# Attention scores: the low parts of the keys in one tile per key-value head, with zeros in the other 64 rows

## The chip, the cores and the metric

The kernel runs on one core of a Trainium2 chip. The metric is the device time of one execution in microseconds (us); of several executions the median is taken. A profiled execution gives, besides, a trace: every instruction of each engine with its start and its length. The engines are PE (TensorE: matmuls, and PEld, the loads of their stationary operand), DVE (VectorE), ACT (ScalarE), POOL (GpSimd) and SP, which here issues the transfers (DMA).

## What is computed

One layer of a decoder for a prompt of 1024 tokens and 8 single-token samples that share the weights. The part that the change touches is the sliding-window attention of the prompt: 8 query heads, 2 key-value heads, 64 channels a head, blocks of 128 queries against the 256 keys of their own and the previous block.

```python
def split_in(h, w_in, q_norm, k_norm):
    z = h @ w_in
    ...
    q = rms_norm(q.reshape(*lead, N_HEADS, HEAD_DIM), q_norm)
    k = rms_norm(k.reshape(*lead, N_KV_HEADS, HEAD_DIM), k_norm)
    ...
def sink_attention(q, k, v, mask, sinks):
    ...
    s = jnp.einsum("nqkgd,nskd->nkgqs", qg, k).astype(jnp.float32) * (HEAD_DIM ** -0.5)
    s = jnp.where(mask, s, NEG)
    ...
    p = jnp.exp(s - m)
    denom = jnp.sum(p, axis=-1, keepdims=True) + jnp.exp(sink - m)
    o = jnp.einsum("nkgqs,nskd->nqkgd", (p / denom).astype(v.dtype), v)
```

Before it stand an RMS norm and the input projection, behind it the gates, the output projection and a SwiGLU.

## The kernel before, in words

Every float32 matrix is kept as a rounded high part and a low part (the remainder), and a product is made of the terms high·high, high·low and low·high. In the helper `mm` (L204 to L211) these are three matmuls that add up in one bank.

The tokens are cut in three chunks of 264, 384 and 384 columns. In the first stage the input is turned (`turn`, L333), its low and high parts go to `hTl` and `hTh`, and a copy `xT` of each turned tile (L345, on ACT) is stored to `xscr` in HBM (L348, issued by SP) for the residual much later. `xT` has a pool of 8 buffers: copy n needs the buffer that the transfer of copy n-8 has read. The norm's factors come from a short chain of POOL operations (`rsqrt`, L115), are spread over the partitions by a matmul (L360) and copied to `bc` by ACT (`norm_bc`, L366). `do_k`, `do_v` and `do_q` multiply their projections by `bc` on DVE (for k: `kr`, L388), and PE turns `kr` (L395, `pkt`).

For attention, `QA[j]` and `QB[j]` hold in one 128-row tile the high part of a query head in the 64 rows of its kv head and the low part in the other 64. `Kh[kv]` holds the key's high part twice, in both halves. `Kl` holds the low parts of both kv heads in one tile, head 0 in rows 0 to 63 and head 1 in rows 64 to 127. So in `att_scores` one matmul with 128 rows (L606) gives q_high·k_high + q_low·k_high, and a second one with 64 rows (L607) adds q_high·k_low.

There are 16 units (8 blocks, 2 kv heads), each with 4 pairs of such matmuls. The table `FILLS` puts groups of 24 matmuls of the projections (`pq`, `pu`, `pg`) between them. A unit goes through scores (PE), mask and maximum (DVE, L610), exponentials (ACT, L616), scaling of the four heads (L622 on POOL, L626 on DVE, L624 on ACT), turning (PE, L634), split in `ph` and `pl` (L214, L215) and products with the values (PE, L651, L652).

What each engine runs in which order is written by a scheduler when the program is made; at run time each engine keeps this order, and a waiting instruction holds up all that stand behind it. SP's transfers take one of eight slots in turn, DMAHW0 to DMAHW7; one waits until the transfer that used its slot before has landed.

Of the kernel before, what the change touches and what calls it, by code (L numbers as in the profile page):

```python
# [7 lines left out]
F32 = mybir.dt.float32  # L8
F32R = mybir.dt.float32r
# [7 lines left out]
P = 128  # L17
# [15 lines left out]
HALF = ((slice(0, 64), slice(64, 128)), (slice(64, 128), slice(0, 64)))  # L33
# [3 lines left out]
def hybrid_step(tc, x_prompt, x_sample, cache_k, cache_v, state_pool, norm1, w_in, q_norm, k_norm, sinks,  # L37
# [4 lines left out]
    V, A, G, T, SP = nc.vector, nc.scalar, nc.gpsimd, nc.tensor, nc.sync  # L42

    def pool(name, bufs=1, side="left", **kw):
        es = ExitStack()
        p = es.enter_context(tc.tile_pool(name=name, bufs=bufs, side=side, reuse_waits="tile", **kw))
        return p, es
# [6 lines left out]
    const, const_es = pool("const")  # L54
# [52 lines left out]
    knc = cols[:, 21:22]  # L107
# [5 lines left out]


    def rsqrt(y, v, n, parts, e):  # L115
        a = const.tile([P, 40], F32, tag="rs_a", bufs=2, name="rs_a")[:parts, :n]
        e.tensor_scalar(y.bitcast(I32), v.bitcast(I32), -0.5, 1597463007.0, op0=ALU.mult, op1=ALU.add)
        for _ in range(3):
            e.tensor_mul(a, y, y)
            if e is V:  # L120
                V.scalar_tensor_tensor(a, a, -0.5, v, ALU.mult, ALU.mult)
                V.scalar_tensor_tensor(y, a, 1.5, y, ALU.add, ALU.mult)
            else:
                e.tensor_mul(a, a, v)
                e.tensor_scalar(a, a, -0.5, 1.5, op0=ALU.mult, op1=ALU.add)
                e.tensor_mul(y, y, a)
# [125 lines left out]
    def unit(p, name, dt=F32):  # L252
        return p.tile([P, NT], dt, tag="u", name=name)
# [9 lines left out]
    bcp, bcp_es = pool("bcp", side="right")  # L263
    bc1 = unit(bcp, "bc1")
    t0p, t0p_es = pool("t0p", bufs=2, side="right")
    kp, kp_es = pool("kp", bufs=3, side="right")
    kvp, kvp_es = pool("kv", side="right")


    Kh = [unit(kp, f"Kh{kv}", F32R) for kv in range(2)]  # L270
    Kl = unit(kp, "Kl", F32R)
    VV = kvp.tile([P, 8, 4, 64], F32R, name="VV")
    st, st_es = pool("st", side="right")

# [58 lines left out]
    def turn(c, tiles, k):  # L333
        c0, N = CH[c]
        pt = bank("pt")
        for n, off, xt in tiles:
            T.transpose(pt[:, off:off + n], xt[:n, k * P:(k + 1) * P], ident[:n, :n])
        hi, lo = hTh[k][:, c0:c0 + N], hTl[k][:, c0:c0 + N]
        turned[c, k] = (A.activation(hi, pt[:, :N], AF.Copy, scale=g1[k]),
                        V.scalar_tensor_tensor(lo, pt[:, :N], g1[k], hi.bitcast(F32), ALU.mult, ALU.subtract))  # L340

        def keep(e=A):
            xT = st.tile([P, 384], F32, tag="xT", bufs=8, name="xT")[:, :N]
            if e is A:
                A.copy(xT, pt[:, :N])  # L345
            else:
                V.tensor_copy(xT, pt[:, :N])
            SP.dma_start(xscr[:, k, c0:c0 + N], xT)  # L348

        return keep  # L350
# [30 lines left out]
    def do_k(ws, c):  # L381
        N, nb, o = CH[c][1], len(CB[c]), (NS if c == 0 else 0)
        b0 = CB[c][0]
        ps = group(ws, hTh, hTl, c, bank("pk"))

        def rest():
            kr = t512("kr")[:, :N]
            V.tensor_mul(kr, ps, bc_of(c))  # L388
            if c == 0:
                V.tensor_copy(qks[:, 4], kr[:, :NS])  # L390

            def token_major():
                pt = bank("pkt")[:, :nb * P]
                for i in range(nb):
                    T.transpose(pt[:, i * P:(i + 1) * P], kr[:, o + i * P:o + (i + 1) * P], ident)  # L395
                sq = t512("ksq")[:, :nb * P]
                A.activation(sq, pt, AF.Square)
                ss = const.tile([P, 8], F32, tag="kss", bufs=2, name="kss")[:, :2 * nb]
                V.reduce_sum(ss, sq.rearrange("p (g d) -> p g d", d=64), axis=AX.X)
                rstd = rstd_of(ss, 2 * nb, 1.0 / 64, "rstdk")  # L400
                kt = t512("kt")[:, :nb * P]
                V.tensor_mul(kt.rearrange("p (g d) -> p g d", d=64), pt.rearrange("p (g d) -> p g d", d=64),
                             rstd.unsqueeze(2).broadcast_to([P, 2 * nb, 64]))
                if CB[c][-1] == 7:
                    nk = t512("nk")[:, :P]
                    V.tensor_mul(nk.rearrange("p (g d) -> p g d", d=64),
                                 kt[:, (nb - 1) * P:nb * P].rearrange("p (g d) -> p g d", d=64),
                                 knb.unsqueeze(1).broadcast_to([P, 2, 64]))
                    SP.dma_start(new_k_prompt[0, 0].rearrange("t h d -> t (h d)"), nk)

                def back():
                    pt2 = bank("pk2")[:, :nb * P]
                    for i in range(nb):
                        T.transpose(pt2[:, i * P:(i + 1) * P], kt[:, i * P:(i + 1) * P], ident)
                    sl = slice(b0 * P, (b0 + nb) * P)
                    for kv, (d, e) in enumerate(HALF):
                        A.activation(Kh[kv][d, sl], pt2[d], AF.Copy, scale=knc[d])
                        V.scalar_tensor_tensor(Kl[d, sl], pt2[d], knc[d], Kh[kv][d, sl].bitcast(F32),
                                               ALU.mult, ALU.subtract)
                        G.tensor_copy(Kh[kv][e, sl], Kh[kv][d, sl])  # L420

                defer(back, 3)

            tick()
            defer(token_major)

        return rest
# [158 lines left out]

    def att_scores(b, kv):
        q0 = NS + P * b
        d = HALF[kv][0]
        k0 = P * max(b - 1, 0)  # L590
        mk = mask[:, 0:256] if b else mask[:, 128:384]
        a = Att()
        a.pr = pr = at.tile([P, 4, 256], F32, tag="p", bufs=3, name="pr")
        mx = at.tile([P, 4], F32, tag="mx", bufs=3, name="mx")
        nm = at.tile([P, 4], F32, tag="nm", bufs=3, name="nm")
        dn = at.tile([P, 4], F32, tag="dn", bufs=3, name="dn")
        es = at.tile([P, 4], F32, tag="es", bufs=3, name="es")
        q_all = (QA, QB)[kv]
        kh = Kh[kv][:, k0:k0 + 256]
        kl = Kl[d, k0:k0 + 256]  # L600
        for jp in range(2):
            s = ptile("s", "s")
            for jj in range(2):
                j = 2 * jp + jj
                sv = s[:, 256 * jj:256 * jj + 256]
                T.matmul(sv, lhsT=q_all[j][:, q0:q0 + P], rhs=kh, start=True, stop=False)  # L606
                T.matmul(sv, lhsT=q_all[j][d, q0:q0 + P], rhs=kl, start=False, stop=True)  # L607
            for jj in range(2):
                j = 2 * jp + jj
                V.tensor_tensor_reduce(pr[:, j], s[:, 256 * jj:256 * jj + 256], mk, op0=ALU.add, op1=ALU.max,  # L610
                                       scale=rq[:, b, kv, j:j + 1], scalar=sinkb[:, 4 * kv + j:4 * kv + j + 1],
                                       accum_out=mx[:, j:j + 1])
        V.tensor_scalar(nm, mx, -1.0, None, op0=ALU.mult)
        V.tensor_sub(es, sinkb[:, 4 * kv:4 * kv + 4], mx)
        for j in range(4):
            A.activation(pr[:, j], pr[:, j], AF.Exp, bias=nm[:, j:j + 1], accum_out=dn[:, j:j + 1])  # L616
        A.activation(es, es, AF.Exp)
        V.tensor_add(dn, dn, es)
        V.reciprocal(dn, dn)
        for j in range(4):  # L620
            if j == 0:
                a.ins = G.tensor_scalar(pr[:, j], pr[:, j], dn[:, j:j + 1], None, op0=ALU.mult)  # L622
            elif j == 3:
                A.activation(pr[:, j], pr[:, j], AF.Copy, scale=dn[:, j:j + 1])  # L624
            else:
                V.tensor_scalar(pr[:, j], pr[:, j], dn[:, j:j + 1], None, op0=ALU.mult)  # L626
        return a

    def att_transpose(b, kv, a):
        a.ph, a.pl = {}, {}  # L630
        for hf in range(min(b + 1, 2)):
            pt = ptile("t", "pt")
            for j in range(4):
                T.transpose(pt[:, P * j:P * j + P], a.pr[:, j, P * hf:P * hf + P], ident)  # L634
            a.ph[hf] = at.tile([P, 512], F32R, tag="ph", bufs=3, name="ph")
            a.pl[hf] = at.tile([P, 512], F32R, tag="pl", bufs=3, name="pl")
            split(a.ph[hf], a.pl[hf], pt)

    yt = [None]
# [319 lines left out]
    for m in range(8):  # L959
# [3 lines left out]
        for c in range(3):  # L963
            c0, N = CH[c]
# [470 lines left out]
    a = {}  # L1435
# [56 lines left out]
```

## Time and profile before

| | us |
|---|---|
| median of 3 runs (1298.44 to 1301.57) | 1300.99 |
| the profiled execution | 1298.46 |
| its span in the trace | 1296.7 |
| PE busy in it (98% of the span) | 1267.9 |
| PEld busy | 1235.9 |
| DVE busy (63%) | 817.9 |
| ACT busy (39%) | 501.2 |
| POOL busy | 52.6 |

"Busy" is the sum of an engine's instructions, overlaps counted once; a matmul's end is modelled, so the distance from start to start of successive matmuls tells more of its price than its length. The mean granted clock of TensorE was 0.996 of full speed.

### The profile page before, as it was taken

How to read it: one execution, taken by the hardware profiler on the slowest of the kernel's cores; microseconds unless marked ns; L12 is line 12 of the kernel's file. 1: busy time of each engine (PE TensorE's matmuls, PEld its weight loads, DVE VectorE, ACT ScalarE, POOL GpSimd, SP SyncE). 2: the span in 40 equal slices, each digit the busy share in tenths (PEclk: the TensorE clock that was granted, in tenths of full speed). 3: DMA queues.
4: the chain of work that ended last, by engine and by line, in shares of the span. 5: the costliest groups of instructions: out<-in, count | busy, mean ns of one | idle time of the engine just before them, and what ended most of it. 6: DMA issues, size and time to landing. Idle time of an engine off the chain costs nothing.

```text
span 1296.7 us, 23776 instructions
## 1 busy us (share of the span) xinstructions
PE 1267.9 (98%) x9436; PEld 1235.9 (95%) x9436; DVE 817.9 (63%) x1600; ACT 501.2 (39%) x980; POOL 52.6 (4%) x191
## 2 busy tenths in 40 slices
PE   7999999999999999996999999999999999999997
PEld 7998888999999999996999999999999999999997
DVE  6768667667344285486865666655667365878642
ACT  6556445452133233454322332223222235334433
POOL 3213101100000000000000000000000000000000
PEclk9999999999999999999999999999999999999999
DMA  7411111211144224655322323223332568847404
GB/s 247 139 29 50 29 34 40 70 50 51 53 143 139 65 74 119 189 150 196 119 93 80 100 97 123 89 84 99 98 123 74 193 184 303 297 172 233 158 25 124
DMA packets 149166, 153.50 MB, mean 118 GB/s; under 512 B 15207, under 2 KB 116263, under 8 KB 149031
## 3 DMA queue, kind: packets, MB, share of 16 engines
q1 hardware_dynamic: 148959, 150.71, 36.8%
q8 instruction: 74, 1.21, 0.4%
q0 software_dynamic: 96, 1.27, 0.2%
q14 instruction: 37, 0.30, 0.1%
HBM read 114.02 MB, written 39.20 MB: 118 GB/s over the span
## 4 chain that ended last, share of the span: by engine, by line
PE 93%; DMA 3%; DVE 2%; SPq 1%; ACT 1%; issue 0%; ACTq 0%; DVEq 0%
PE py L1131 5%; PE py L1133 5%; PE py L1132 5%; PE pg L209 5%; PE pg L210 5%; PE pg L211 5%; PE pz L1131 3%; PE pz L1132 3%; PE px L1133 3%; PE pz L1133 3%; PE px L1131 3%; PE px L1132 3%; PE dy L1131 2%; PE dy L1132 2%; PE pw L209 2%; PE pw L211 2%
## 5 line engine op out<-in xcount | busy, mean ns | idle before, releaser
L209 PE MATMUL pg<-hTh,whi 128*128 128x384 f32 (+1 forms) x384 | 123.4, 322 | 0.0
L210 PE MATMUL pg<-hTl,whi 128*128 128x384 f32 (+1 forms) x384 | 123.1, 321 | 0.0
L211 PE MATMUL pg<-hTh,wlo 128*128 128x384 f32 (+1 forms) x384 | 122.7, 320 | 0.0
L138 ACT CAST whi<-wraw 128x512 fp32r<-128x512 f32 x102 | 63.0, 620 | 135.6 <-PE pa L210 31.3
L139 DVE TENSOR_TENSOR wlo<-wraw,whi 128x512 fp32r<-128x512 f32 x102 | 70.1, 687 | 71.4 <-ACT whi L138 63.8
L138 ACT CAST whi<-t 128x512 fp32r<-128x512 f32 x80 | 49.4, 621 | 154.0 <-PE py L1132 82.8
L138 ACT CAST whi<-raw 128x512 fp32r<-128x512 f32 x60 | 37.3, 621 | 114.7 <-PE px L1132 65.9
L1131 PE MATMUL dy<-ah,whi 128*128 128x258 f32 x264 | 75.0, 284 | 0.0
L1132 PE MATMUL dy<-al,whi 128*128 128x258 f32 x264 | 75.0, 284 | 0.0
L1133 PE MATMUL dy<-ah,wlo 128*128 128x258 f32 x264 | 74.7, 284 | 0.0
L209 PEld LDWEIGHTS pg<-hTh,whi 128*128 128x128 f32 x384 | 72.2, 188 | 1.1 <-DVE t L822 0.2
L210 PEld LDWEIGHTS pg<-hTl,whi 128*128 128x128 f32 x384 | 72.1, 188 | 0.9
L211 PEld LDWEIGHTS pg<-hTh,wlo 128*128 128x128 f32 x384 | 72.0, 188 | 0.4
L209 PE MATMUL pw<-mh,whi 128*128 128x258 f32 x256 | 72.4, 283 | 0.0
L210 PE MATMUL pw<-ml,whi 128*128 128x258 f32 x256 | 72.0, 282 | 0.0
L211 PE MATMUL pw<-mh,wlo 128*128 128x258 f32 x256 | 72.0, 282 | 0.0
L139 DVE TENSOR_TENSOR wlo<-raw,whi 128x512 fp32r<-128x512 f32 x60 | 41.1, 684 | 36.0 <-ACT whi L138 30.9
L138 ACT CAST whi<-H 128x512 fp32r<-128x512 f32 x55 | 33.8, 620 | 65.6 <-PE dy L1132 22.7
L215 DVE TENSOR_TENSOR al<-ar,ah 128x1032 fp32r<-128x1032 f32 (+1 forms) x42 | 47.9, 1141 | 15.4 <-ACT ah L214 15.3
L139 DVE TENSOR_TENSOR wlo<-t,whi 128x512 fp32r<-128x512 f32 x80 | 54.1, 683 | 3.0 <-ACT whi L138 3.0
L1131 PE MATMUL px<-c1h,whi 128*128 128x258 f32 x172 | 49.4, 287 | 6.0 <-ACT whi L138 6.0
L214 ACT CAST ah<-ar 128x1032 fp32r<-128x1032 f32 (+1 forms) x42 | 41.3, 982 | 25.5 <-DMA ar<-s 25.4
(445 smaller groups left out, 4450.0 us busy)
## 6 DMA issues: line engine op xcount, KB each, us to landing
ar<-s SPq DMA_DIRECT2D x35, 516.0 KB
d<-in_w_down_dram SPq DMA_DIRECT2D x44, 256.0 KB
s<-g SPq DMA_DIRECT2D x40, 258.0 KB
wraw<-in_w_in_dram SPq DMA_DIRECT2D x40, 256.0 KB
raw<-in_w_gate_dram SPq DMA_DIRECT2D x20, 512.0 KB
raw<-in_w_up_dram SPq DMA_DIRECT2D x20, 512.0 KB
wraw<-in_w_out_dram SPq DMA_DIRECT2D x32, 256.0 KB
s<-fs SPq DMA_DIRECT2D x30, 258.0 KB
```

Of the source, the lines that this page charges most:

```text
L138: mark["act"] = A.copy(hi, raw)
L139: mark["dve"] = e.tensor_sub(lo, raw, hi.bitcast(F32))
L209: T.matmul(ps, lhsT=wh, rhs=xh, start=(k == 0), stop=False)
L210: T.matmul(ps, lhsT=wh, rhs=xl, start=False, stop=False)
L211: T.matmul(ps, lhsT=wl, rhs=xh, start=False, stop=(k == n - 1))
L214: A.copy(hi, src)
L215: e.tensor_sub(lo, src, hi.bitcast(F32))
L1131: T.matmul(ps, lhsT=wh, rhs=ah, start=start, stop=False, skip_group_check=True)
L1132: T.matmul(ps, lhsT=wh, rhs=al, start=False, stop=False, skip_group_check=True)
L1133: T.matmul(ps, lhsT=wl, rhs=ah, start=False, stop=stop, skip_group_check=True)
```

## The change

`Kl` becomes two tiles, one per kv head, with the low part in the head's 64 rows and zeros in the other 64; the zeros are written once by POOL at the program's start. The second score product then takes all 128 rows of the query tile and of `Kl[kv]`; the zeros take out the part that isn't wanted. The tile costs 4 KB more per partition, and three pools give up buffers for it: `rs_a` (scratch of `rsqrt`) goes from 2 to 1, `xT` from 8 to 6, `pl` from 3 to 2.

```diff
     def rsqrt(y, v, n, parts, e):
-        a = const.tile([P, 40], F32, tag="rs_a", bufs=2, name="rs_a")[:parts, :n]
+        a = const.tile([P, 40], F32, tag="rs_a", bufs=1, name="rs_a")[:parts, :n]
...
-    kp, kp_es = pool("kp", bufs=3, side="right")
+    kp, kp_es = pool("kp", bufs=4, side="right")
...
-    Kl = unit(kp, "Kl", F32R)
+    Kl = [unit(kp, f"Kl{kv}", F32R) for kv in range(2)]
+    for kv in range(2):
+        G.memset(Kl[kv][HALF[kv][1]].bitcast(F32), 0.0)
...
-            xT = st.tile([P, 384], F32, tag="xT", bufs=8, name="xT")[:, :N]
+            xT = st.tile([P, 384], F32, tag="xT", bufs=6, name="xT")[:, :N]
...
-                        V.scalar_tensor_tensor(Kl[d, sl], pt2[d], knc[d], Kh[kv][d, sl].bitcast(F32),
+                        V.scalar_tensor_tensor(Kl[kv][d, sl], pt2[d], knc[d], Kh[kv][d, sl].bitcast(F32),
...
     def att_scores(b, kv):
         q0 = NS + P * b
-        d = HALF[kv][0]
...
-        kl = Kl[d, k0:k0 + 256]
+        kl = Kl[kv][:, k0:k0 + 256]
...
                 T.matmul(sv, lhsT=q_all[j][:, q0:q0 + P], rhs=kh, start=True, stop=False)
-                T.matmul(sv, lhsT=q_all[j][d, q0:q0 + P], rhs=kl, start=False, stop=True)
+                T.matmul(sv, lhsT=q_all[j][:, q0:q0 + P], rhs=kl, start=False, stop=True)
...
-            a.pl[hf] = at.tile([P, 512], F32R, tag="pl", bufs=3, name="pl")
+            a.pl[hf] = at.tile([P, 512], F32R, tag="pl", bufs=2, name="pl")
```

The order of PE's instructions is the same, one for one, as before. The order on the other engines differs in the first stage alone. On ACT, where the turned copies of chunk 0 end and `bc` of that chunk is made, stood before (`xT_333` and `xT_336` are the copies of tiles 6 and 7; a wait on DMAHWn is one on the transfer in that slot):

```order
L318 ACTIVATE junk_414,ss_413<-xr_180 128x1024 [waits DMAHW3_49,DMAHW2_49,Activation_49]
L345 COPY xT_333<-pt_281 128x264 [waits DVE_49]
L180 CAST qwh_437<-qw_196 128x8x64 [waits DMAHW6_49]
L180 CAST qwh_437<-qw_198 128x8x64 [waits DMAHW7_49]
L345 COPY xT_336<-pt_290 128x264 [waits DVE_49]
L366 COPY bc1_144<-pb_347 128x264 [waits PE_49]
L397 ACTIVATE ksq_386<-pkt_383 128x256 [waits DVE_49,PE_49]
```

and now (line numbers are two higher; the copies of tiles 6 and 7 are `xT_336` and `xT_339`):

```order
L320 ACTIVATE junk_417,ss_416<-xr_183 128x1024 [waits DMAHW3_49,DMAHW2_49,Activation_49]
L180 CAST qwh_440<-qw_199 128x8x64 [waits DMAHW6_49]
L180 CAST qwh_440<-qw_201 128x8x64 [waits DMAHW7_49]
L347 COPY xT_336<-pt_284 128x264 [waits DMAHW0_49,DVE_49]
L347 COPY xT_339<-pt_293 128x264 [waits DMAHW2_49,DVE_49]
L368 COPY bc1_144<-pb_350 128x264 [waits PE_49]
L399 ACTIVATE ksq_389<-pkt_386 128x256 [waits DVE_49,PE_49]
```

Both copies have moved behind the two casts of `qwh`, to just ahead of `bc`, and both now wait for a transfer. Which transfers these are shows on SP, where the stores of the first copies (`xT_281`, `xT_290`: tiles 0 and 1) take the slots DMAHW0 and DMAHW2. SP's queue of the change from there, which up to this place is in the order of before:

```order
L99 DMA knb_110<-in_k_norm_dram 128x64 [waits DMAHW7_49]
L350 DMA xscr_118<-xT_281 128x264 [waits DMAHW0_49,Activation_49]
L101 DMA sink64_111<-in_sinks_dram 8x1 [waits DMAHW1_49]
L350 DMA xscr_118<-xT_290 128x264 [waits DMAHW2_49,Activation_49]
L350 DMA xscr_118<-xT_299 128x264 [waits DMAHW3_49,Activation_49]
```

So the copy of tile 6 waits for the store of tile 0, and the copy of tile 7 for the store of tile 1. On POOL the two chains of `rsqrt` for chunk 1, that of the keys (`rstdk`) and that of the input's norm (`rstd1`), stood interleaved:

```order
L119 TENSOR_TENSOR rs_a_393<-rstdk_391 128x4 [waits Pool_49]
L119 TENSOR_TENSOR rs_a_423<-rstd1_421 128x3 [waits Pool_49]
L124 TENSOR_TENSOR rs_a_393<-rs_a_393,rs_v_390 128x4 [waits Pool_49]
L124 TENSOR_TENSOR rs_a_423<-rs_a_423,rs_v_420 128x3 [waits Pool_49]
L125 TENSOR_SCALAR rs_a_393<-rs_a_393 128x4 [waits Pool_49]
```

and now the chain of the keys runs to its end first:

```order
L119 TENSOR_TENSOR rs_a_396<-rstdk_394 128x4 [waits Pool_49]
L124 TENSOR_TENSOR rs_a_396<-rs_a_396,rs_v_393 128x4 [waits Pool_49]
L125 TENSOR_SCALAR rs_a_396<-rs_a_396 128x4 [waits Pool_49]
L126 TENSOR_TENSOR rstdk_394<-rstdk_394,rs_a_396 128x4 [waits Pool_49]
L119 TENSOR_TENSOR rs_a_396<-rstdk_394 128x4 [waits Pool_49]
```

All twelve operations of `rstdk` have moved ahead of the twelve of `rstd1`; chunk 2 reads the same.

## Rows read from the trace of the kernel before

**Rows 1.** Busy us: stretch, length, PE, PEld, DVE, ACT, POOL; clock; DMA; GB/s.

```profile
20.00:76.00 56.00, 55.44 (x367) 53.54 (x366) 40.25 (x86) 35.48 (x75) 13.71 (x71) 1.00 0.43 132
90.00:150.00 60.00, 60.00 (x334) 51.35 (x333) 46.87 (x159) 34.98 (x105) 18.07 (x53) 1.00 0.13 39
150.00:246.00 96.00, 96.00 (x554) 83.11 (x553) 65.80 (x226) 48.42 (x146) 9.30 (x13) 1.00 0.12 35
246.00:600.00 354.00, 352.80 (x2458) 350.58 (x2456) 200.99 (x388) 128.17 (x235) 1.79 (x4) 1.00 0.38 113
```

**Rows 2.** Instructions in order of time, one unit's scores on PE and PEld.

```profile
96.45 0.18 PEld L607 LDWEIGHTS s<-Kl,QB 64*128 64x128 f32 x1 [0.19 <-issue]
96.46 0.38 PE L607 MATMUL s<-Kl,QB 64*128 64x256 f32 x1
...
96.77 0.39 PE L606 MATMUL s<-Kh,QB 128*128 128x256 f32 x1
...
97.08 0.38 PE L607 MATMUL s<-Kl,QB 64*128 64x256 f32 x1
```

**Rows 3.** The same view in a projection group: matmuls of 128 rows alone.

```profile
206.00 0.28 PE L209 MATMUL pg<-hTh,whi 128*128 128x264 f32 x1
206.01 0.19 PEld L210 LDWEIGHTS pg<-hTl,whi 128*128 128x128 f32 x1
206.12 0.29 PE L210 MATMUL pg<-hTl,whi 128*128 128x264 f32 x1
```

**Rows 4.** One line's instructions: count, ns least/median/most, first and last start.

```profile
L607 PE MATMUL s<-Kl,QA x32: 379/381/391, 79.5 to 225.3; 64*128 64x256 f32 x32
```

**Rows 5.** Instructions in order of time on ACT, 20 to 27 us.

```profile
20.15 0.38 ACT L345 COPY xT<-pt 128x264 f32<-128x264 f32 x1
20.42 0.38 ACT L366 COPY bc<-pb 128x264 f32<-128x264 f32 x1
...
26.27 1.29 ACT L345 COPY xT<-pt 128x384 f32<-128x384 f32 x3 [1.19 <-DMA xscr<-xT]
```

**Rows 6.** The same view on SP's queue: stores of `xT` from tile 1 on.

```profile
21.94 1.68 SPq L348 DMA_DIRECT2D xscr<-xT  x3
```

**Rows 7.** The same view: what follows `bc` on DVE and PE.

```profile
20.89 0.43 DVE L388 TENSOR_TENSOR kr<-pk,bc 128x264 f32<-128x264 f32 x1
...
21.37 0.33 PE L395 MATMUL pkt<-ident,kr 128*128 128x128 f32 x1 [0.27 <-DMA xr<-in_x_prompt_dram]
```

**Rows 8.** PE in order of time: its longest idle time.

```profile
615.49 0.58 PE L1131 MATMUL px<-c1h,whi 128*128 128x258 f32 x1 [5.43 <-ACT whi L138]
```

**Rows 9.** Busy time per stretch around it, columns as in the first group.

```profile
610.00:620.00 10.00, 3.53 (x15) 3.16 (x15) 10.00 (x12) 5.58 (x7) 0.00 (x0) 0.72 0.11 32
620.00:625.00 5.00, 4.98 (x37) 4.78 (x37) 4.99 (x8) 4.24 (x8) 0.00 (x0) 0.88 0.59 198
```

**Rows 10.** In order of time: unit 0's last scaling, and its turn.

```profile
104.36 0.49 ACT L624 ACTIVATE pr<-pr,dn 128x256 f32<-128x256 f32 x1
...
109.04 0.27 PE L634 MATMUL pt<-ident,pr 128*128 128x128 f32 x1
```

**Rows 11.** In order of time: a `pl`, and the product two before.

```profile
204.75 0.47 PE L652 MATMUL py<-pl,VV 128*128 128x512 f32 x1
...
205.64 0.69 DVE L215 TENSOR_TENSOR pl<-pt,ph 128x512 fp32r<-128x512 f32 x1
```

**Rows 12.** In order of time on POOL: start, and chunk 1's chains.

```profile
1.21 0.43 POOL L79 MEMSET mask<- 128x384 f32 x1
...
9.06 0.19 POOL L117 TENSOR_SCALAR rstd<-rs_v 128x3 int32<-128x3 int32 x1 [3.81 <-DVE rs_v L131]
...
23.54 0.20 POOL L119 TENSOR_TENSOR rs_a<-rstdk 128x4 f32<-128x4 f32 x1
...
27.11 0.19 POOL L126 TENSOR_TENSOR rstd<-rstd,rs_a 128x3 f32<-128x3 f32 x1
```

**Rows 13.** In order of time on DVE: where chunk 1's factor is read.

```profile
31.24 0.54 DVE L358 TENSOR_TENSOR dg<-ident,rstd 128x384 f32<-128x384 f32 x1
```

## The prediction

> **What bounds the kernel now.** I read the windows first, to see in which stage the change lies and what bounds it. The scores run from 79 to 236 us [rows 4]. From 90 to 246 us PE is busy in 156 of 156 us, and it is nearly so on both sides (55.4 of 56 us before, 352.8 of 354 us behind), while DVE has 78% and ACT 58% in the busiest stretch [rows 1]. So PE's stream of instructions is the time, and what a matmul costs is the distance to the start of the next one. Then I read PE and PEld in order of time. In a unit's scores the starts lie 0.31 us apart, and the load for the 64-row matmul begins after 0.19 us in which PEld waited for nothing that the profile shows [rows 2]. In a projection group, with 128 rows throughout, matmuls of 264 columns (8 more than the scores have) start 0.12 us apart although each has its own load of 0.19 us: the next load runs beside the matmul [rows 3]. So the extra 0.19 us stands at each change between 128 and 64 rows. Last I read the first stage, because there the order of ACT changes: ACT, SP, then what hangs on them.
>
> **The score products.** There are 64 matmuls of 64 rows (32 on QA, 32 on QB, which reads alike) [rows 4], and each stands between two of 128 rows: 128 changes of 0.31 - 0.12 = 0.19 us, 24.3 us. By pairs: 0.31 + 0.31 = 0.62 us [rows 2] against 2 x 0.12 [rows 3], 0.38 us, times 64 is 24.3 again. After the change both products have the form of a projection matmul with 256 columns. At 0.115 us apiece it would be 25 us, no more; the lower end is nothing, if loads of the same query tile in quick succession don't hide. I take **-24.3 us**, since the nearest rows are nearly the same form.
>
> TensorEngine Tiling (Array Packing) of the Trainium skill, Key Properties, says that changing the tiling mode drains the engine, and counts 64 rows as such a mode; the 0.19 us ahead of the load agree. TensorE: Matmul & The Clock Gate of the Trainium skill, Part 3 (what overlaps and what doesn't), says that a load overlaps a matmul in flight only when their row groups differ, which speaks against the change: by it two 128-row products would be the worst case. The loads of the projections, which run beside matmuls of the same 128 rows, disagree with it here; by the first rule the sum is as above, by the second the 24.3 us would be missing.
>
> **Whether the units keep up.** PE's gain is real only if softmax is ready sooner too. From 90 to 150 us stand seven units with 28 pairs, so PE would need 60 - 28 x 0.38 = 49.4 us, and DVE has 46.9 us of work there [rows 1]: 95%. DVE would have to lose most of its idle time; at worst, if it lost none, 10.6 us of the gain go. But PE turns a unit's weights late: unit 0's last scaling ends at 104.85 us, the turn that reads it starts at 109.04 us, 4.2 us later [rows 10]. By then PE has gained three units, 4.6 us, and DVE and ACT perhaps half of that, so the slack shrinks to 2 us or so. Later units have more. From 150 us on, PE would need 96 - 12.2 = 83.8 us against 65.8 us of DVE [rows 1]. I take **+1 us**, with 0 and 10.6 as ends.
>
> **The stores of `xT`.** With 6 buffers the copies of tiles 6 and 7 wait for the stores of tiles 0 and 1, and they now stand right ahead of `bc` on ACT. The store of tile 1 is issued at 21.94 us [rows 6]; SP's order up to there hasn't changed, so it will be again. When it lands, the trace of before tells, since copy 9 (the second of chunk 1) needs the same buffer with 8: ACT waited 1.19 us for that transfer and began at 26.27 us [rows 5]. So the copy of tile 7 begins at 26.27 us, not at 20.15, and `bc` at 26.54, not at 20.42 [rows 5]. Behind `bc` waits `kr` on DVE, and behind that `pkt` on PE, at 21.37 us [rows 7]; PE's order is kept, so all that follows waits as well, though the turns of chunk 1 don't need it. The shift is 26.27 - 20.15 = 6.1 us, and as PE is the bound up to 76 us [rows 1] and further, nothing gives it back. If the last part of the store lands sooner, it is less, but not under 1.8 us, since the store isn't issued before 21.94 us [rows 6]; one that lands a microsecond later makes it 7. I take **+6.1 us**.
>
> PE then idles from 21.10 to 27.5 us, 6.4 us. In its one idle time of such length, 5.43 us [rows 8], the granted clock fell: 0.72 of full over 610 to 620 us and 0.88 over the next 5 us [rows 9] are 5.6 and 1.2 us at half, that is at 1.2 GHz instead of 2.4, until about 621.2 us and so for 5.7 us after PE had begun again. Half of 5.7 is 2.9 us lost at most; if the clock doesn't fall, nothing. I take **+2.6 us**, nearer to the one case that the trace has. This lag of PE also covers that DVE now makes the low parts of a query tile (two instructions) ahead of chunk 1's last `hTl`.
>
> **The rest, at nothing.** Two memsets of 64x1032 on POOL: 0.43 us for 384 columns [rows 12] gives some 1.2 us each, and POOL idles 3.8 us ahead of 9.06 us [rows 12]; without that cover the norm of chunk 0 would be late by as much. `rs_a` with one buffer: in chunk 1 both chains ran together from 23.54 to 27.30 us; one behind the other, the second ends at most 3.8 us later, at 31.1 us [rows 12], and DVE read it at 31.24 us [rows 13], behind work that shifts with PE. `pl` with two buffers: a `pl` may begin when the product with the second last one is done; at the tightest place that I saw, the product ends at 205.22 us and the `pl` begins at 205.64 us [rows 11], both in the order of before, and PE is ahead of before by as much as DVE or more. The writes of `Kl` are as many as before.
>
> **The sum.** The profiled execution took 1298.46 us: 1298.46 - 24.3 + 1 + 6.1 + 2.6 = 1283.9. It lies 0.2% under the median of the runs, inside their spread of 3 us; I say **1284 us**. About 0.3%, 4 us, is what a measurement of this kernel can tell from no change.
>
> **The rivals.**
> - The first stage is hardly held up: the stores of tiles 0 and 1 land as soon as they are issued, at some 22 us, and PE is held up by 2 us, too short a time for the clock to fall. For it speaks only that I have one landing to go by; against it that ACT waited for just this transfer until 26.2 us [rows 5]. 1298.46 - 24.3 + 1 + 2 = 1277 us. Chance 0.10.
> - DVE becomes the bound from 90 to 150 us: 95% is close, and its order mixes waits for PE, ACT and POOL. Against it stands the 4.2 us of slack. 1284 + 9.6 = 1293 us. Chance 0.10.
> - Slower: the two loads of 128 rows don't hide, because the same query tile is loaded twice in a row into the full array while a product of the same rows is in flight. Then a score product still costs 0.31 us, nothing is gained, and the delay of the first stage is left: 1298.46 + 8.7 = 1307 us. The point from which it decides is a distance of 0.31 - 8.7/128 = 0.24 us. Against it: in a projection L209 and L210 load the same tile twice in just this way [rows 3]. The rule on row groups in TensorE: Matmul & The Clock Gate of the Trainium skill, Part 3, would have it so; those rows disagree with it. This is also the case in which the change doesn't do what it says. Chance 0.04.
>
> **How the numbers follow.** My forecast has the other 0.76; its own range is 1278 to 1290: no fall of the clock, 25 us of gain and a somewhat earlier landing at one end, 3 us more waits and the baseline at its median at the other. With the first rival, less 2 us for no waits at all in the units, and part of the second, the range is 1275 to 1291. Only the third case lies above 1297 us, so faster has 0.94, the same 0.02 and slower 0.04.
>
> **What would show it.** Starts 0.12 us apart in the scores, with PEld never idle ahead of L608; an ACT wait of 1 us and more for the store of `xT` ahead of `bc`, a `pkt` at 27.5 us, PE idle for 6 us ahead of it and a clock under 1 behind it; between 76 and 246 us the stage shorter by 23 to 24 us. It would be wrong if PE waits for DVE for many us between 90 and 150 us, or if PE reaches `pkt` at 21 to 24 us.

## The result, and the profile after

The changed kernel takes 1284.25 us (median of 4 runs, 1281.08 to 1284.95) against 1300.76 us for the kernel before: 16.5 us less by the medians. The ratio is 0.9867, 95% interval 0.9855 to 0.9879; it is an estimate over the executions, here and below, and not the quotient of the two medians, which is 0.9873. Medians below leave out two executions in a slow state, 1369.13 us in `e7_all64` and 4292.74 us in `e6_issue`. Its profiled execution took 1284.43 us, with a span of 1282.7 us. All lines of the code now stand one or two lower: the score products are L607 and L608, the copy to `xT` L347, its store L350, `bc` L368, `kr` L390, `pkt` L397.

The page's line of busy time, shares of the span and instructions of each engine:

```profile
PE 1248.0 (97%) x9436; PEld 1233.9 (96%) x9436; DVE 817.3 (64%) x1600; ACT 501.4 (39%) x980; POOL 55.9 (4%) x193
```

PE is still the engine whose work is the time. Then the scores, a unit in order of time on PE, and a load from PEld:

```profile
102.14 0.28 PE L607 MATMUL s<-Kh,QB 128*128 128x256 f32 x1
102.25 0.28 PE L608 MATMUL s<-Kl,QB 128*128 128x256 f32 x1
102.37 0.28 PE L607 MATMUL s<-Kh,QB 128*128 128x256 f32 x1
...
102.14 0.19 PEld L608 LDWEIGHTS s<-Kl,QB 128*128 128x128 f32 x1
```

Starts lie 0.12 us apart where they lay 0.31 us apart [rows 2]. The load of the low product still takes 0.19 us, but it begins with the matmul ahead of it and waits for nothing: the bracket with 0.19 us of "issue" is gone.

How long the scores last is read from PE's rows at their two ends. Of the kernel before:

```profile
79.06 0.29 PE L606 MATMUL s<-Kh,QA 128*128 128x256 f32 x1
...
236.19 0.44 PE L209 MATMUL pg<-hTh,whi 128*128 128x384 f32 x1
```

And of the kernel after:

```profile
86.50 0.28 PE L607 MATMUL s<-Kh,QA 128*128 128x256 f32 x1
...
219.64 0.35 PE L209 MATMUL pg<-hTh,whi 128*128 128x384 f32 x1
```

From the first score to the matmul behind the last one it was 157.13 us and is now 133.14 us: 24.0 us less. But the scores begin 7.4 us later. Where that comes from is in the first stage; ACT, SP's queue, DVE and PE in order of time:

```profile
24.96 0.85 ACT L347 COPY xT<-pt 128x264 f32<-128x264 f32 x2 [4.18 <-DMA xscr<-xT]
25.70 0.39 ACT L368 COPY bc<-pb 128x264 f32<-128x264 f32 x1
...
22.24 1.67 SPq L350 DMA_DIRECT2D xscr<-xT  x3
...
26.12 0.43 DVE L390 TENSOR_TENSOR kr<-pk,bc 128x264 f32<-128x264 f32 x1 [4.62 <-ACT bc L368]
...
26.61 0.69 PE L397 MATMUL pkt<-ident,kr 128*128 128x128 f32 x2 [6.20 <-DVE kr L390]
```

ACT stands 4.18 us for a store of `xT`, `bc` comes at 25.70 us instead of 20.42 us [rows 5], and PE stands 6.20 us ahead of `pkt`, which begins at 26.61 us instead of 21.37 us [rows 7]. What that does to the clock is in the busy time per stretch (columns as in [rows 1]):

```profile
20.00:30.00 10.00, 3.80 (x20) 3.23 (x18) 3.50 (x11) 3.54 (x8) 1.06 (x6) 0.62 0.70 231
30.00:35.00 5.00, 5.00 (x35) 4.98 (x33) 2.35 (x5) 2.68 (x8) 3.53 (x19) 0.74 0.83 219
...
90.00:150.00 60.00, 60.00 (x401) 59.15 (x400) 51.26 (x173) 38.59 (x111) 20.97 (x60) 1.00 0.17 47
```

A clock of 0.62 over 10 us and of 0.74 over 5 us is 7.6 and 2.6 us at 1.2 GHz instead of 2.4. The last row is the stretch in which DVE might have become the bound: PE is busy in all 60 us, DVE in 51.26.

So the difference is -24.0 us in the scores and +7.4 us ahead of them: PE is through with them at 219.64 us instead of 236.19 us, 16.6 us sooner, which is about what the medians differ by. The spans of the two profiled executions differ by 14.0 us only; the other 2.6 us lie behind the scores, where nothing was changed. The sums of three windows each, of before from 236.2 us to the end and of after from 219.6 us (length, then busy time):

```profile
sum 1060.50, PE 1039.15 PEld 1032.56 DVE 652.19 ACT 370.72 POOL 2.74; mean PE 346.38 PEld 344.19 DVE 217.40 ACT 123.57 POOL 0.91
```

```profile
sum 1063.10, PE 1041.46 PEld 1034.81 DVE 652.84 ACT 370.78 POOL 3.72; mean PE 347.15 PEld 344.94 DVE 217.61 ACT 123.59 POOL 1.24
```

With the same matmuls PE is busy 2.3 us longer, which is the clock: in this execution of after it was 0.66 of full from 237 to 242 us (last section), where before has no fall, and 0.90 in the 50 us from 565 us, where before has 0.93 in the 50 us from 580 us. Together that is some 7 us more at half clock, about 3 us lost at most.

### The profile page after: what moved, and what is told of

The parts are those of the page before. It is cut to its first block, busy times and chain, and to the rows that moved or that the text cites. A ratio compares the mean times of both kernels' runs of the same rounds, so it can differ in the third digit from the quotient of the medians.

```text
span 1282.7 us, 23784 instructions
## 1 busy us (share of the span) xinstructions
PE 1248.0 (97%) x9436; PEld 1233.9 (96%) x9436; DVE 817.3 (64%) x1600; ACT 501.4 (39%) x980; POOL 55.9 (4%) x193
## 4 chain that ended last, share of the span: by engine, by line
PE 93%; DMA 4%; DVE 2%; SPq 0%; ACT 0%; issue 0%; ACTq 0%; DVEq 0%
PE py L1132 5%; PE py L1134 5%; PE py L1133 5%; PE pg L211 5%; PE pg L209 5%; PE pg L210 5%; PE pz L1132 3%; PE pz L1133 3%; PE px L1134 3%; PE pz L1134 3%; PE px L1132 3%; PE px L1133 3%; PE dy L1132 2%; PE pw L209 2%; PE dy L1133 2%; PE dy L1134 2%
## 5 line engine op out<-in xcount | busy, mean ns | idle before, releaser
L138 ACT CAST whi<-t 128x512 fp32r<-128x512 f32 x80 | 49.4, 621 | 153.8 <-PE py L1133 79.0
L139 DVE TENSOR_TENSOR wlo<-H,whi 128x512 fp32r<-128x512 f32 x55 | 37.5, 688 | 21.5 <-ACT whi L138 20.4
```

The costliest lines, as they stand in the source:

```text
L138: mark["act"] = A.copy(hi, raw)
L139: mark["dve"] = e.tensor_sub(lo, raw, hi.bitcast(F32))
```

## The experiments

The theory was that of the prediction: 0.19 us for each change between 64 and 128 rows, and a stall of the first stage by the stores of `xT`, with a fall of the clock behind it. The rivals were that the gain of the scores is smaller and the first stage costs nothing, and that 64 rows cost 0.31 us wherever they stand. Medians of the kernel before were 1300.75 to 1301.32 us beside these runs.

**The buffers of `xT` alone** (`e1_stores`), in the kernel before:

```
-            xT = st.tile([P, 384], F32, tag="xT", bufs=8, ...
+            xT = st.tile([P, 384], F32, tag="xT", bufs=6, ...
```

> The kernel before with 6 buffers for xT instead of 8, and nothing else; the scores keep their 64 rows. Theory (the copies of tiles 6 and 7 wait for stores ahead of bc, PE stands 5 to 6 us before pkt and its clock falls): 1300.8 + 5.2 of shift (what the trace of the changed kernel shows) + about 2.6 of clock = 1308 to 1309 us, ratio 1.006. Rival (the stores are no matter and the scores gained only some 16 us): within 2 us of the kernel before, 1301 to 1303 us.

Measured: 1310.13 us, ratio 1.0069 (1.0056 to 1.0083), 9.4 us more (7.3 to 10.8). ACT and PE in order of time:

```profile
25.43 0.72 ACT L345 COPY xT<-pt 128x264 f32<-128x264 f32 x2 [4.79 <-DMA xscr<-xT]
...
26.94 0.69 PE L395 MATMUL pkt<-ident,kr 128*128 128x128 f32 x2 [5.78 <-DVE kr L388]
```

The two buffers alone cost all that the changed kernel loses ahead of its scores (7.4 us in its trace). The rival of a smaller gain falls.

**Everything but the product** (`e2_rows64`), from the kernel after:

```
-        kl = Kl[kv][:, k0:k0 + 256]
+        kl = Kl[kv][d, k0:k0 + 256]
...
-                T.matmul(sv, lhsT=q_all[j][:, q0:q0 + P], rhs=kl, start=False, stop=True)
+                T.matmul(sv, lhsT=q_all[j][d, q0:q0 + P], rhs=kl, start=False, stop=True)
```

> The changed kernel with the second score product back on the 64 rows that hold the low parts; buffers, memsets and the two low-part units stay as changed. Theory (24.3 us of the scores at the row changes, everything else at nothing but the stores): 1284.2 + 24.3 = 1308.5 us, the same as the run before it in this list. Rival (the scores gained only some 16 us net and nothing was lost): 1301 us. Rival (the rest, memsets or the buffers of the rsqrt and of the weights, costs as well): more than 1.5 us above the run with 6 buffers alone.

Measured: 1308.36 us, ratio 1.0062 (1.0048 to 1.0076). That is 24.1 us above the kernel after, the price of the 128 changes, and not above the run with the buffers alone: memsets, low-part units and the other two buffers cost nothing that shows.

**Eight buffers again** (`e3_xt8`), in the kernel after, the two more taken from units that are free in the first stage:

```
-            xT = st.tile([P, 384], F32, tag="xT", bufs=6, name="xT")[:, :N]
+            xT = (unit(t0p, "xT") if k > 5 else st.tile([P, 384], F32, tag="xT", bufs=6, name="xT"))[:, :N]
```

> The changed kernel with two more buffers for xT, taken from the two units that the attention stage uses later, for tiles 6 and 7 of every chunk; so a copy waits for the same store as with 8. Theory: no wait ahead of bc, pkt at 20 to 21.5 us, no idle time of 6 us and no fall of the clock there: 1284.2 - 5.2 - 3 = 1276 us, ratio 0.981 of the kernel before. Rival (bc is late for another reason, or what is gained there is given back by a wait in the attention stage, where DVE is close): 1281 us and more.

Measured: 1276.55 us, ratio 0.9821 (0.9804 to 0.9838): 24.2 us under the kernel before and 7.7 us under the changed one (6.0 us by the two ratios). It beats both. ACT and PE in order of time, and the stretch in which DVE is closest:

```profile
20.05 0.37 ACT L347 COPY xT<-pt 128x264 f32<-128x264 f32 x1
20.32 0.38 ACT L368 COPY bc<-pb 128x264 f32<-128x264 f32 x1
...
21.35 0.38 PE L397 MATMUL pkt<-ident,kr 128*128 128x128 f32 x2
...
90.00:150.00 60.00, 60.00 (x403) 58.62 (x403) 51.32 (x176) 39.59 (x118) 17.79 (x48) 1.00 0.15 43
```

`bc` and `pkt` stand where they stood before the change, and nothing of the 24 us is given back to a wait for softmax.

**Fewer changes with as many products of 64 rows** (`e4_regroup`), in the kernel before:

```
-                T.matmul(sv, lhsT=q_all[j][:, q0:q0 + P], rhs=kh, start=True, stop=False)
-                T.matmul(sv, lhsT=q_all[j][d, q0:q0 + P], rhs=kl, start=False, stop=True)
+                if jj == 0:
+                    T.matmul(sv, lhsT=q_all[j][:, q0:q0 + P], rhs=kh, start=True, stop=False)
+                T.matmul(sv, lhsT=q_all[j][d, q0:q0 + P], rhs=kl, start=jj == 1, stop=jj == 0)
+                if jj == 1:
+                    T.matmul(sv, lhsT=q_all[j][:, q0:q0 + P], rhs=kh, start=False, stop=True)
```

> The kernel before, with the products of every second head in the other order, low part first: full, 64, 64, full instead of full, 64, full, 64. As many matmuls of each kind, but 64 changes of the rows instead of 128. Theory (0.19 us at each change, in either direction): half of 24.3 us less, 1300.8 - 12.2 = 1288.6 us, starts 0.31, 0.12, 0.31, 0.12 apart. Rival (the load of a 64-row matmul never hides, nor the load right behind one): only the load between two full products hides, 32 x 0.19 = 6 us less, 1294.7 us. Rival (the 64-row product itself takes 0.31 us, wherever it stands): 1288.6 us too, but with starts 0.31, 0.31, 0.12, 0.12 apart counted from the 64-row ones.

Measured: 1290.85 us, ratio 0.9923 (0.9908 to 0.9937), 9.9 us less (8.2 to 12.0). PE in order of time, two heads (L608 is the product of 64 rows, twice):

```profile
103.41 0.28 PE L607 MATMUL s<-Kh,QA 128*128 128x256 f32 x1
103.62 0.50 PE L608 MATMUL s<-Kl,QA 64*128 64x256 f32 x2
104.04 0.39 PE L610 MATMUL s<-Kh,QA 128*128 128x256 f32 x1
104.27 0.49 PE L485 MATMUL pqt<-ident,qsq 128*128 128x128 f32 x3
```

Four products take 0.86 us, as 2 x 0.31 + 2 x 0.12 does, where four took 4 x 0.31 = 1.24 us; but the starts are not 0.31 and 0.12 apart. They are 0.21, two in 0.42, and 0.23: the price of a change that stands alone is spread over its own start and the next. The trace of before has 132 changes between 64 and 128 rows in all and this one 74, because the order of PE put other turns between some products; 58 x 0.19 = 11 us, inside the interval. The two ends of the scores in this trace say it more sharply:

```profile
79.37 0.29 PE L607 MATMUL s<-Kh,QA 128*128 128x256 f32 x1
...
225.89 0.34 PE L209 MATMUL pg<-hTh,whi 128*128 128x384 f32 x1
```

That is 146.52 us against 157.13 us for the same matmuls in another order: 10.6 us for 58 changes, 0.18 us each. The end at 6 us, that no load next to 64 rows hides, is outside of the interval.

**64 rows throughout** (`e7_all64`), in the kernel after; the second product is edited in the same way:

```
-        kh = Kh[kv][:, k0:k0 + 256]
+        kh = Kh[kv][d, k0:k0 + 256]
...
-                T.matmul(sv, lhsT=q_all[j][:, q0:q0 + P], rhs=kh, start=True, stop=False)
+                T.matmul(sv, lhsT=q_all[j][d, q0:q0 + P], rhs=kh, start=True, stop=False)
```

> The changed kernel with both score products on the 64 rows of the high parts' half; it leaves out the product of the queries' low parts with the keys' high parts. The row changes are then only at the ends of some 31 stretches of scores, about 62 instead of 128. Theory (0.19 us belongs to a change of the rows, not to 64 rows): matmuls of 64 rows behind one another start 0.12 us apart, and the time is 1284.2 + 62 x 0.19 = 1296 us. Rival (a 64-row product costs 0.31 us by itself): 0.31 us between all starts in the scores, 1284.2 + 24.3 = 1308.5 us.

Measured: 1296.81 us, ratio 0.9961 (0.9949 to 0.9974), 12.6 us above the kernel after. PE in order of time:

```profile
102.75 0.39 PE L608 MATMUL s<-Kh,QB 64*128 64x256 f32 x1
102.97 0.28 PE L609 MATMUL s<-Kl,QB 64*128 64x256 f32 x1
103.09 0.28 PE L608 MATMUL s<-Kh,QB 64*128 64x256 f32 x1
103.21 0.28 PE L609 MATMUL s<-Kl,QB 64*128 64x256 f32 x1
103.42 0.44 PE L487 MATMUL pqt<-ident,qsq 128*128 128x128 f32 x2
...
85.83 0.38 PE L608 MATMUL s<-Kh,QA 64*128 64x256 f32 x1
...
231.70 0.44 PE L209 MATMUL pg<-hTh,whi 128*128 128x384 f32 x1
```

Behind one another, products of 64 rows start 0.12 us apart. What costs is the change: 0.22 us behind the first of the stretch and 0.21 us behind the last. This trace has 74 changes, 70 more than the kernel after; 12.6 us over 70 is 0.18 us each (the interval of the ratio reaches from 0.14 to 0.19). The last two lines shown are the ends of the scores: 145.87 us against 133.14 us in the kernel after, 12.7 us, again 0.18 us each.

**The clock by itself** (`e5_fill`), in the kernel after:

```
                 pt = bank("pkt")[:, :nb * P]
+                if c == 0:
+                    for _ in range(44):
+                        T.matmul(pt, lhsT=wk[0][0], rhs=hTh[0][:, :nb * P], start=True, stop=True)
```

> The changed kernel with 44 extra matmuls of 256 columns ahead of the turn pkt, in the bank that pkt overwrites; they compute nothing that is used and should take some 44 x 0.115 = 5 us of the 6.2 us in which PE stands idle there. Theory (the idle time, not the late start, makes the clock fall to 0.5 behind it, and that costs about 2.2 us: the scores began 7.45 us later than in the kernel before, 5.24 of them from pkt's start): no fall at 22 to 33 us, pkt as late as without the filling, 1284.2 - 2.2 = 1282 us. Rival (the clock falls in this place anyway, or the fall costs nothing): 1284 us and more, with half clock at the same place.

Measured: 1282.67 us, ratio 0.9859 (0.9844 to 0.9874). The interval holds the kernel after too, so the time alone tells nothing; the trace does. Nine of the 44 extra matmuls ran earlier, from 18.4 us on; the other 35 and `pkt` on PE, the same stretches as above, and the line of the first score product (first and last start):

```profile
22.16 4.28 PE L398 MATMUL pkt<-hTh,whi 128*128 128x256 f32 x35
27.74 0.44 PE L400 MATMUL pkt<-ident,kr 128*128 128x128 f32 x2 [1.30 <-DVE kr L390]
...
20.00:30.00 10.00, 8.70 (x73) 8.30 (x72) 3.05 (x10) 3.19 (x8) 0.48 (x3) 1.00 0.66 225
30.00:35.00 5.00, 5.00 (x43) 4.98 (x42) 3.42 (x10) 4.28 (x11) 3.52 (x19) 1.00 0.96 261
...
L610 PE MATMUL s<-Kh,QA x32: 275/280/365, 85.1 to 209.0; 128*128 128x256 f32 x32
```

In this execution the store landed 1.2 us later still, and `pkt` began at 27.74 us. Even so the scores begin 1.4 us sooner, because the clock stays at full: from `pkt` to the first score it is 57.4 us, against 59.9 us in the kernel after and 57.7 us in the kernel before. The fall of the clock cost 2.2 to 2.5 us, and it was the idle time that made it fall. The other traces agree: between 20 and 35 us the clock was at half for 6.8 to 10.2 us in the four kernels whose PE stood 5.5 to 6.2 us ahead of `pkt` (the kernel after, `e1_stores`, `e2_rows64`, `e7_all64`), with 59.1 to 60.5 us from `pkt` to the first score; it stayed at full in the five in which PE stood there for 1.2 us at most (the kernel before, `e3_xt8`, `e4_regroup`, `e8_rest`, `e10_both`), with 57.1 to 57.7 us.

**Stores issued by ACT** (`e6_issue`), in the kernel after:

```
-            SP.dma_start(xscr[:, k, c0:c0 + N], xT)
+            (A if c == 0 and k < 2 else SP).dma_start(xscr[:, k, c0:c0 + N], xT)
```

> The changed kernel, 6 buffers for xT, with the stores of tiles 0 and 1 of the first chunk issued on ACT's queue, behind their copies at some 10 to 11 us, instead of on SP's, where they stood behind loads until 20.9 and 22.24 us. Theory (it is SP's late issue that makes the stores late): they land long before 19 us, no wait ahead of bc, and the time is that with 8 buffers, 1276.5 us, or up to 1 us more for two issues on ACT. Rival (the transfer itself is slow behind the loads of the other chunks): the copies of tiles 6 and 7 still wait for several us, 1280 to 1284 us.

Measured: 1285.74 us, ratio 0.9882 (0.9867 to 0.9898): neither. ACT and its queue in order of time, then SP's queue, then the line of the store on ACT's queue:

```profile
10.79 0.38 ACT L347 COPY xT<-pt 128x264 f32<-128x264 f32 x1
21.31 0.34 ACTq L350 DMA_DIRECT2D xscr<-xT  x1
21.70 0.48 ACT L341 ACTIVATE hTh<-pt,cols 128x264 fp32r<-128x264 f32 x1 [10.52 <-DMA xr<-in_x_prompt_dram]
...
15.99 3.27 SPq L308 DMA_DIRECT2D xr<-in_x_prompt_dram  x6
...
L350 ACTq EVENT_SEMAPHORE  x2: 17/17/17, 21.3 to 22.7; - x2
```

The issue of the store stood 10.5 us on ACT, until a load of tokens had landed, and everything behind it on ACT stood with it (PE for 14.9 us). So it isn't SP's queue that makes the stores late. The wait is the one on a slot (DMAHW0 in SP's order): the store of tile 0 may be issued when the transfer eight before it has landed, which here is the first of chunk 2's six loads, issued at 15.99 us, with two small loads behind them. On ACT that wait is an instruction of its own (EVENT_SEMAPHORE at 21.3 us, right ahead of the issue). Another queue doesn't change the slot; it only puts the wait on ACT. My theory on this point fell, and the rival's time came by another way than it had.

**The loads behind the stores** (`e9_loads`), in the kernel after:

```
-    tl.append(norm_load(2))
...
+    with behind(0, 7):
+        tl.append(norm_load(2))
     ek = do_k(wk, 0)
```

> The changed kernel, 6 buffers for xT, with the six loads of chunk 2's tokens issued on SP behind the first stores of xT instead of ahead of them (3.4 us of issues and 1.5 MB that the stores now stand behind); one issue behind another there waits for loads to land. Theory (it is the loads ahead that make the stores late): the stores of tiles 0 and 1 are issued at 16 to 18 us and land by 20 us, bc is at 20 to 21 us, and the time is that with 8 buffers, 1276.5 us, up to 2 us more if the projection weights or chunk 2's tokens are late. Rival (the stores are late whatever stands ahead of them): bc at 25 to 26 us, 1284 us.

Measured: 1279.19 us, ratio 0.9836 (0.9820 to 0.9851). SP's queue, ACT and PE in order of time, and the clock:

```profile
18.50 2.33 SPq L350 DMA_DIRECT2D xscr<-xT  x3
...
21.08 0.78 ACT L347 COPY xT<-pt 128x264 f32<-128x264 f32 x2 [4.73 <-DMA xscr<-xT]
21.76 1.14 ACT L180 CAST qwh<-qw 128x512 fp32r<-128x512 f32 x2
22.80 0.38 ACT L368 COPY bc<-pb 128x264 f32<-128x264 f32 x1
...
24.10 0.44 PE L397 MATMUL pkt<-ident,kr 128*128 128x128 f32 x2 [1.98 <-DVE kr L390]
...
24.00:30.00 6.00, 5.90 (x36) 5.71 (x37) 4.07 (x13) 3.52 (x8) 3.06 (x16) 0.72 0.95 296
```

With 1.5 MB of loads behind them the stores are issued 3.7 us sooner, and the copies go on 3.9 us sooner: the loads ahead were most of the lateness, not all of it. The order of ACT had changed too, so that `bc` now stands behind two casts. **Both mends together** (`e10_both`) were expected so:

> The same with the two more buffers for xT as well, so that no copy waits for a store. If the stores alone made bc late, it is no faster than either of the two mends by itself: 1276.5 us, within 1.5 us. If the order of loads has a worth of its own (the projection weights land sooner), 1274 us; if chunk 2's tokens come late, 1278 us and more.

Measured: 1277.79 us, ratio 0.9825 (0.9809 to 0.9841), no better than the buffers alone.

**The other two buffers** (`e8_rest`), in the kernel before:

```
-        a = const.tile([P, 40], F32, tag="rs_a", bufs=2, ...
+        a = const.tile([P, 40], F32, tag="rs_a", bufs=1, ...
...
-            a.pl[hf] = at.tile([P, 512], F32R, tag="pl", bufs=3, ...
+            a.pl[hf] = at.tile([P, 512], F32R, tag="pl", bufs=2, ...
```

> The kernel before with one buffer for the scratch of the rsqrt (rs_a) and two for the low parts of the weights (pl), and nothing else. Theory (both at nothing): 1300.8 us, within the measurement. Rival (the two chains on POOL or the turned weights now wait): 2 us and more above, with a wait for rs_a in the first stage or for pl in the scores.

Measured: 1302.0 us, ratio 1.0004 (0.9994 to 1.0014): nothing.

## Why the prediction was right

**The score products**, -24.3 us: right. The scores and what stands between them take 24.0 us less, the run without the product alone is 24.1 us above the kernel after, and the one without the stall is 24.2 us under the kernel before. That the price belongs to the change of rows is shown from two sides, with as many products of 64 rows but fewer changes, and with more products of 64 rows and fewer changes. The rule on row groups in TensorE: Matmul & The Clock Gate of the Trainium skill, Part 3, would have left all starts at 0.31 us; loads of 128 rows beside matmuls of the same rows, 0.12 us apart, disagree with it, and so do the products of 64 rows of one half. The rule of TensorEngine Tiling (Array Packing) of the Trainium skill, Key Properties, that a change of the mode drains the engine, agrees with both runs.

**Whether the units keep up**, +1 us: nothing to pay. 24.0 of 24.1 to 24.3 us arrive at the end of the scores, and PE waits for nothing between 76 and 225 us. The rival that DVE becomes the bound falls: it has 51.3 us of work in 60 us where I feared 46.9 of 49.4. My 95% took DVE's busiest stretch for the whole: from the first score to the matmul behind the last it has 110.85 us of work in 157.13 us before and 109.11 in 133.14 us now, 82%.

**The stores of `xT`**, +6.1 us: the chain was right link by link (store, copy, `bc`, `kr`, `pkt`), the size a little high: `pkt` is 5.24 us later. The landing was taken from one execution, where a copy began at 26.27 us; in three others the copies went on at 24.96, at 25.43 and (with the filling) at 26.18 us. So the term is uncertain by about 0.6 us to either side, whatever is read.

**The fall of the clock**, +2.6 us: 2.2 to 2.5 us in the profiled execution. The times from `pkt` to the first score in the other runs give an estimate of 1.4 us at the least (`e7_all64`) and 3.4 us at the most (`e1_stores`).

**The sum** held by two errors that cancel. I made it from an execution that lay 2.3 us under the median of the runs, and my terms gave -14.6 us where the runs gave -16.5. From the median with my terms it would have been 1286.2 us. That 1284 us was hit to 0.3 us is luck; the mechanism of the two large terms, and their sizes to within 1 us, are not.

**The rest at nothing**: right, by two runs. The memsets of `Kl` took 0.95 us each, and the norm behind them began as before, its cover down from 3.81 us [rows 12] to 2.73 us:

```profile
3.46 0.95 POOL L273 MEMSET Kl<- 64x1032 f32 x1
...
9.01 0.19 POOL L117 TENSOR_SCALAR rstd<-rs_v 128x3 int32<-128x3 int32 x1 [2.73 <-DVE rs_v L131]
```

**The rival of a short stall** had its mechanism wrong in one place: I held 2 us of idle time for too short to bring the clock down. In the trace of before that is so twice: PE stood 2.00 us ahead of 602.17 us and 2.20 us ahead of 608.36 us, and the clock was 1.00 until 614 us. In `e9_loads` it is not: PE stood 1.98 us, then ran only turns until 26.05 us, and the clock was 0.94 from 24 to 26 us and 0.50 from 26 to 28 us. Idle time of that length decides nothing by itself.

## What to carry to other kernels

Where matmuls of two row counts alternate and PE is the bound, padding the smaller with zeros to the larger costs nothing by itself and saves the price of the changes, 0.18 to 0.19 us each here; where padding is not possible, put those of one row count behind one another. Look at where the room for the padding comes from: two buffers given up in another stage cost a third of the gain, and two units that were idle there gave it back. To price a buffer, follow its oldest reader (here a store) to the end of its transfer, with the earlier transfer whose slot it needs, and then list what stands behind the waiting instruction on its engine.

## What I had not expected of the hardware

- A change of rows that stands alone doesn't show as one start of 0.31 us: the start behind it and the next come 0.21 to 0.23 us apart, each some 0.1 us late. Only when changes follow each other directly is every start 0.31 us apart.
- The issue of a store on ACT stood 10.5 us until a load had landed. That is the program's own wait for a slot, and not shown to be the chip's doing; an engine that issues a transfer among many loads takes this wait on itself, ahead of all its other work.
- The clock fell with PE busy throughout (columns as above, kernel after; the first line is PE in order of time):

```profile
234.88 1.95 PE L790 MATMUL pY<-pz,cv 128*128 128x8 f32 x16
...
230.00:237.00 7.00, 7.00 (x49) 6.64 (x48) 1.82 (x4) 0.57 (x5) 1.14 (x3) 1.00 0.53 196
237.00:242.00 5.00, 5.00 (x21) 4.76 (x20) 3.63 (x15) 2.64 (x14) 0.00 (x0) 0.66 0.10 36
```

  0.66 of 5 us is 3.4 us at half, 1.7 us lost. What PE did just ahead was 2 products of 64 columns and 16 of 8 columns, from 234.52 to 236.69 us. Such a fall begins 0.4 to 1.1 us behind the start of the last of these products in nine of the twelve traces; in the kernel before (1.00 in [rows 1]), `e9_loads` and `e10_both` the same products run and nothing falls. That the products bring it about is not shown, since no run leaves them out or moves them. Falls like this are part of why executions of one kernel spread: of the kernel after, the one of 1281.08 us had a mean clock of 0.992 and the one of 1284.95 us had 0.986.
- The clock on record can be missing at the start of a trace. Of the kernel before (columns as above):

```profile
13.00:15.00 2.00, 2.00 (x10) 1.97 (x10) 1.86 (x6) 2.00 (x7) 0.03 (x1) 1.00 0.35 127
```

  The clock is given as 1.00, but from 13.41 us on matmuls of 264 columns start 0.22 us apart, and at full clock they start 0.12 us apart [rows 3]. The kernel after has the same 0.22 us in the same place with a clock of 0.50 on record. So a 1.00 in the first 17 us of the trace of before, and its mean of 0.996, say less than the distances between starts.
